# Layer A's attention: the value products that close a unit are issued ahead of a step's scores

## The chip, the cores and the metric

The kernel runs on one core of a Trainium2 chip. The metric is the device time of one execution in microseconds (us). Three runs of the kernel before gave 2460.7 (median), 2458.39 and 2463.78 us.

## The reference, cut to what matters

The reference is a two-layer decoder trunk over 2048 tokens of width 1024. The change lies in the first layer's attention: 16 heads of width 64, causal, with a learned forget gate whose cumulative logarithm is added to the logits:

```python
logits = einsum('bqhd,bkhd->bhqk', qi, k) * scale
logits = logits + ci[..., :, None] - c_k[..., None, :]
logits = where(causal, logits, -inf)
p = softmax(logits, axis=-1)
out = einsum('bhqk,bkhd->bqhd', p, v)
```

Before it stands a projection of the normed input to queries, keys, values, forget logits and a gate; after it the gated output projection and the second layer.

## The kernel before, in words

All products are made with fp32 operands split into a high and a low part. The first layer's attention is a generator, `attention_a`. Its work is cut into **units**, one for each head and each chunk of 512 queries: 16 heads by 4 chunks is 64 units. A unit of chunk ch (0 to 3) has 2·ch + 2 **steps** of two key blocks of 128, so the chunks have 2, 4, 6 and 8 steps, a head has 20 and all heads 320. The last two steps of a unit lie on the diagonal and are masked; the very last one is only 256 + 128 queries wide.

For each step n the main loop (L1132 on) issues, in this order:

1. `ahead(target - 1)` and later `ahead(target)`: **max pieces** for a chunk about 14 steps on. A piece is one or two products on TensorE (L936) into the tile `mx`, of which there is one, and a row maximum on VectorE: L952 for the first half of a long row, L947 (with the mask, and a short read of the accumulator) for the second. The four maxima of a chunk go by DMA into a row of the query operand (L560). There are 24 pieces to a head, so a step has one, or now and then two.
2. `scores(n)`: four products (L984, L985) into two of three `sc` banks, on diagonal steps the mask products (L989, L993); the exponential on ScalarE (L990, L999); its high part, also on ScalarE (L1002); the low part by a subtraction on GpSimd (L1003); and sums of the exponentials into `ac` on VectorE (L1012; at the first step of a unit a ScalarE copy, L1006, takes the place of one addition; at its end L897 reduces `ac`).
3. `values(...)` of the oldest pending step, three steps back (`V_LAG = 3`): four products (L1027) of the high and low parts with the values, which add up in the one `pa` bank over the unit. The last `values` of a unit also issues the **output copy** from `pa` on ScalarE (L1035) and two DMAs on SyncE's queue that store it (L1037, L1038). Only when the copy is over can the next unit's first value product write to `pa`.
4. `recips`, five steps after a head's end: a small product (L906) and its reciprocals.
5. `feed`: some products of the SiLU gate's projection (L1066) into the `pb` bank, which fill up TensorE.

So after a unit's last step k, its closing values are issued at step k + 3, and the first values of the next unit at step k + 4. By the chunk that ends, step k + 3 is the third step of chunk 1 (after chunk 0), the third step of chunk 2, the third step of chunk 3, and, after chunk 3, the first step of chunk 1 of the next head.

Each engine works through its own queue in order. The order in the queues is laid down when the program is built, by and large in the order of issue, with what was not expected to be ready moved back. `sq` has two buffers, shared by the output copy, the gate's results and the reciprocals.

Of the kernel before, what the change touches and what calls it, by code (L numbers as in the profile page):

```python
# [40 lines left out]
V_LAG = 3  # L41
# [57 lines left out]
def f_(ap):  # L99
    return ap.bitcast(F32)  # L100
# [51 lines left out]
class Trunk:  # L152
# [696 lines left out]
    def attention_a(self, op):  # L849
# [19 lines left out]
        units = [(h, ch) for h in range(H) for ch in range(NCH)]  # L869
# [24 lines left out]
        def sums(u):  # L894

            h, ch = units[u]
            nc.vector.tensor_reduce(  # L897
                part[:, h % 2, ch, :], state[u][0].rearrange("p (b i) -> p b i", i=32),
                AX.X, ALU.add, apply_transpose=True,
            )  # L900

        def recips(h, c0=0, c1=NCH):

            nr = (c1 - c0) * NSB
            ps = self.ps("sc", [nr, 32])
            nc.tensor.matmul(  # L906
                ps, part[:, h % 2, c0:c1].rearrange("p c b -> p (c b)"), self.fold,
                start=True, stop=True,
            )
            rc = self.sb("sq", [nr, 32])  # L910
            nc.vector.tensor_tensor(rc, ps, roots[:nr, 1 if c0 else 0], ALU.mult)
            nc.vector.reciprocal(rc, rc)
            nc.sync.dma_start(
                out=d["rd"][h, c0 * CH : c1 * CH].rearrange("(b i) -> b i", i=32), in_=rc
            )
# [44 lines left out]
        def blocks(ch, p):  # L960

            if p < 2 * ch:
                return [(2 * p, 0, 512, 0), (2 * p + 1, 0, 512, 512)]
            if p == 2 * ch:
                return [(2 * p, 0, 512, 0), (2 * p + 1, 128, 384, 512)]
            return [(2 * p, 256, 256, 0), (2 * p + 1, 384, 128, 256)]

        def scores(n, u, p):
            h, ch = units[u]
            ka, kb, qa, qb, v, _ = heads[h]  # L970
            bl = blocks(ch, p)
            diag, last = p >= 2 * ch, p > 2 * ch

            tiles = [self.ps("sc", [P, CH]) for _ in range(1 if last else 2)]
            tw = bl[1][3] + bl[1][2]
            pf = self.sb("st", [P, 1024])
            ph, pl = pht[:, n % 4, :], plt[:, n % 4, :]
            for n_, (k, q0, w, off) in enumerate(bl):
                qs = slice(ch * CH + q0, ch * CH + q0 + w)
                ks = slice(k * P, (k + 1) * P)  # L980
                ps = tiles[0 if last else n_]
                o0 = off if last else 0
                o = ps[:, o0 : o0 + w]
                nc.tensor.matmul(o, ka[:, ks], qa[:, qs], start=not (last and n_), stop=False)  # L984
                nc.tensor.matmul(o, kb[:, ks], qb[:, qs], start=False, stop=not diag)  # L985

            if last:
                o = tiles[0].rearrange("p (b q) -> p b q", b=2)[:, :, :P]
                nc.tensor.matmul(o, self.identb, self.mask_s, start=False, stop=True)  # L989
                nc.scalar.activation(pf[:, :tw], tiles[0][:, :tw], AF.Exp, scale=HD**-0.5)  # L990
            else:
                for n_, ps in enumerate(tiles if diag else ()):
                    mm = nc.tensor.matmul(  # L993
                        ps[:, :P], self.identb, self.mask_s[:, 0], start=False, stop=True
                    )
                    if n_:
                        tc.keep_in_program_order(mm)
                for ps, (k, q0, w, off) in zip(tiles, bl):
                    nc.scalar.activation(  # L999
                        pf[:, off : off + w], ps[:, :w], AF.Exp, scale=HD**-0.5  # L1000
                    )
            nc.scalar.copy(ph[:, :tw], pf[:, :tw])  # L1002
            nc.gpsimd.tensor_tensor(pl[:, :tw], pf[:, :tw], f_(ph[:, :tw]), ALU.subtract)  # L1003
            if p == 0:
                state[u] = [self.ps("ac", [P, CH]), None]
                nc.scalar.copy(state[u][0], pf[:, :CH])  # L1006
            acc = state[u][0]
            for n_, (k, q0, w, off) in enumerate(bl):
                if p == 0 and n_ == 0:
                    continue  # L1010
                a_ = acc[:, q0 : q0 + w]
                nc.vector.tensor_tensor(a_, a_, pf[:, off : off + w], ALU.add)  # L1012
            if last:
                sums(u)
            return (u, p, ph, pl)

        def values(item):
            u, p, ph, pl = item
            h, ch = units[u]
            v = heads[h][4]  # L1020
            if p == 0:
                state[u][1] = self.ps("pa", [P, CH])
            pv = state[u][1]
            last = p == 2 * ch + 1
            for n_, (k, q0, w, off) in enumerate(blocks(ch, p)):
                for i, src in enumerate((ph, pl)):
                    nc.tensor.matmul(  # L1027
                        pv[:, q0 : q0 + w], v[:, k, :], src[:, off : off + w],
                        start=(p == 0 and n_ == 0 and i == 0),
                        stop=(last and n_ == 1 and i == 1),  # L1030
                    )
            if last:
                state.pop(u)
                ov = self.sb("sq", [P, CH])
                nc.scalar.copy(ov, pv)  # L1035
                rows, cols = slice(h * HD, (h + 1) * HD), slice(ch * CH, (ch + 1) * CH)
                nc.sync.dma_start(out=d["om"][rows, cols], in_=ov[:HD, :])  # L1037
                nc.sync.dma_start(out=d["oc"][rows, cols], in_=ov[HD:, :])  # L1038

        def gate_weights(ft, dt):  # L1040
            w = self.sb(next(weight_slots), [P, 2, 2, 2, P], F32R)
            nc.sync.dma_start(out=f_(w), in_=d["wg"][ft, :, dt // 2 : dt // 2 + 2])
            return w
# [39 lines left out]
        def more_pieces(n):  # L1083
            nonlocal loaded
            while len(pieces) < n and loaded < H:
                load_max(loaded)
                if loaded:
                    load_rest(loaded)
                for ch in range(NCH):
                    pieces.extend(max_pieces(loaded, ch))  # L1090
                loaded += 1
# [8 lines left out]
        def ahead(target):  # L1100
            nonlocal done
            while done < min(target, len(pieces)):
                pieces[done]()
                done += 1
# [11 lines left out]
        def feed(n, pause=False):  # L1116


            nonlocal fed, rest
            if pause and rest:  # L1120
                rest = False
                return
            while fed < min(total, n):
                next(filler, None)
                fed += 1
                if pause and fed % (3 * NDT) == 0:
                    rest = True
                    break

        pending, due = [], []  # L1130

        for n, (u, p) in enumerate(steps):  # L1132
            h, ch = units[u]
            if n % per_head == LOAD_AT and h + 1 < H:
                more_pieces(len(pieces) + 1)
            target = per * (n + AHEAD + 1) // per_head + 1
            ahead(target - 1)
            pending.append(scores(n, u, p))
            ahead(target)
            if len(pending) > V_LAG:  # L1140
                values(pending.pop(0))
            if p == 2 * ch + 1:
                if h == H - 1 and ch in (0, NCH - 1):
                    due.append((n + SUM_LAG, (h, ch and 1, ch + 1)))
                elif ch == NCH - 1:
                    due.append((n + SUM_LAG, (h,)))
            while due and due[0][0] <= n:
                recips(*due.pop(0)[1])
            feed((total - KEPT) * (n + 1) // len(steps), pause=True)
            if n == RAW_AT:  # L1150
                raw = self.sb("big", [P, NDT // 2, D])
                for p in range(NDT // 2):
                    op.weight_load(p, raw[:, p])
            if n in PREP_AT:
                op.load(PREP_AT.index(n), ("qn", "wh", "qn", "wl"))
                op.prepare(PREP_AT.index(n), nc.gpsimd)
# [466 lines left out]
```

## Time and profile before

| | |
|---|---|
| median of the runs | 2460.7 us (2458.39 to 2463.78) |
| profiled execution, first to last instruction | 2459.7 us |
| its main attention stage | about 599 to 1462 us |
| TensorE (PE) busy | 2424.1 us, 12016 products |
| weight loads (PEld) busy | 2022.4 us |
| VectorE (DVE) busy | 1727.4 us |
| ScalarE (ACT) busy | 1255.1 us |
| GpSimd (POOL) busy | 1001.9 us |
| TensorE clock granted, mean | 0.999 |

The profile gives one row for each group of instructions: source line, engine, operation, output and input tiles, shape, count, then busy time, mean duration, and the idle time of the engine ahead of them with what ended most of it. A product is given from its start to a modelled end, and the next one may start before that end; so the distance between two starts, not the length, is what a product takes of TensorE's time. A timeline row merges like instructions that follow each other (x4 is four of them) and states the start, the length to the end of the last, and, in brackets, idle time and who ended it.

### The profile page before, as it was taken

The page shows a single profiled execution, that of the slowest core. Times are in us where ns is not written, and L with a number is a line of the kernel's source. Part 1 is how long each engine was busy: PE and PEld are TensorE (multiplying, and loading weights), DVE is VectorE, ACT ScalarE, POOL GpSimd, SP SyncE. Part 2 cuts the span into 40 slices and gives each one's busy share as a digit, 9 for nine tenths or more (in the row PEclk, how much of TensorE's full clock was granted, in tenths as well). Part 3 has the DMA queues.
Part 4 walks back from the last instruction along what each step waited for, and adds up shares of the span by engine and source line. Part 5 has one row for each costly group of instructions (what it writes and reads, how often), then busy time and mean ns, then how long its engine had stood idle before and what let it go on. Part 6 is the DMA issues. An engine that isn't in the chain of part 4 may idle for free.

```text
span 2459.7 us, 36240 instructions
## 1 busy us (share of the span) xinstructions
PE 2424.1 (99%) x12016; PEld 2022.4 (82%) x12016; DVE 1727.4 (70%) x3826; ACT 1255.1 (51%) x2504; POOL 1001.9 (41%) x643
## 2 busy tenths in 40 slices
PE   8999999999999999999999999999999999999999
PEld 6788899988888887878877778888788888888887
DVE  7656567735888888888888866456766523777776
ACT  5433324323777777777777761135323312555554
POOL 0000000012877777777778862210011000377775
PEclk9999999999999999999999999999999999999999
DMA  6656545687554655465456649975434415555552
GB/s 181 207 165 193 156 145 168 192 261 223 168 155 128 210 141 150 143 198 164 133 168 182 169 137 306 290 253 153 139 90 120 137 64 165 174 176 178 180 180 73
DMA packets 351515, 419.24 MB, mean 170 GB/s; under 512 B 64928, under 2 KB 248256, under 8 KB 345152
## 3 DMA queue, kind: packets, MB, share of 16 engines
q1 hardware_dynamic: 351328, 416.92, 56.6%
q8 instruction: 95, 1.56, 0.3%
q14 instruction: 92, 0.75, 0.1%
HBM read 265.29 MB, written 151.40 MB: 169 GB/s over the span
## 4 chain that ended last, share of the span: by engine, by line
PE 46%; DVE 4%; DMA 2%; ACT 2%; POOL 2%; issue 2%; SPq 0%; DVEq 0%; ACTq 0%; POOLq 0%
PE b L759 9%; PE b L1240 5%; PE pa L1027 5%; PE pb L1453 4%; PE pb L722 3%; PE pb L1066 3%; PE b L722 3%; PE mx L936 2%; PE sc L985 2%; PE sc L984 2%; PE pa L1383 1%; PE b L1304 1%; PE pa L722 1%; PE pa L1240 1%; PE pb L1240 1%
## 5 line engine op out<-in xcount | busy, mean ns | idle before, releaser
L759 PE MATMUL b<-wh,big 128*128 128x512 f32 (+3 forms) x2560 | 770.1, 375 | 9.8 <-ACT wh L486 8.7
L1003 POOL TENSOR_TENSOR big<-st,big 128x1024 fp32r<-128x1024 f32 (+1 forms) x320 | 657.9, 2070 | 261.4 <-ACT big L1002 155.6
L759 PEld LDWEIGHTS b<-wh,big 128*128 128x128 f32 x2560 | 471.3, 188 | 81.2 <-ACT wh L486 10.5
L759 PE MATMUL b<-wl,big 128*128 128x512 f32 (+3 forms) x1280 | 474.2, 371 | 1.9 <-DVE wl L487 1.9
L1012 DVE TENSOR_TENSOR ac<-ac,st 128x512 f32<-128x512 f32 (+3 forms) x576 | 355.4, 617 | 55.6 <-ACT st L999 27.2
L999 ACT ACTIVATE st<-sc 128x512 f32<-128x512 f32 (+1 forms) x512 | 274.3, 585 | 161.8 <-PE sc L985 79.0
L1027 PE MATMUL pa<-big 128*128 128x512 f32 (+3 forms) x1280 | 326.1, 369 | 3.9 <-POOL big L1003 1.8
L1002 ACT CAST big<-st 128x1024 fp32r<-128x1024 f32 (+1 forms) x320 | 295.6, 924 | 7.8
L759 PEld LDWEIGHTS b<-wl,big 128*128 128x128 f32 x1280 | 241.4, 189 | 38.3 <-DVE wl L487 6.1
L1027 PEld LDWEIGHTS pa<-big 128*128 128x128 f32 x1280 | 222.0, 189 | 50.3 <-ACT sq L1035 17.0
L947 DVE CUSTOM_DVE_ANT_0 mx<-mx,rot 128x128 f32<-128x128 f32 (+3 forms) x240 | 210.7, 878 | 40.9 <-PE mx L936 34.8
L495 ACT ACTIVATE sq<-b,r 128x512 f32<-128x512 f32 (+2 forms) x128 | 77.8, 608 | 301.6 <-PE b L759 298.6
L984 PE MATMUL sc<-big 128*128 128x512 f32 (+3 forms) x640 | 230.1, 364 | 1.3 <-DVE st L542 1.1
L985 PE MATMUL sc<-big 67*128 67x512 f32 (+3 forms) x640 | 229.0, 367 | 0.0
L936 PE MATMUL mx<-big 66*128 66x128 f32 (+3 forms) x660 | 191.1, 363 | 3.6 <-DVE mt L947 3.1
L1066 PE MATMUL pb<-wh,wr 128*128 128x512 f32 x488 | 179.3, 398 | 2.8 <-DMA wr<-wg 2.2
L859 POOL MEMSET rot<- 128x1024 bf16 x1 | 1.0, 952 | 420.8 <-PE pb L349 420.8
L497 DVE TENSOR_REDUCE sm<-sq 128x8 f32<-128x512 f32 (+2 forms) x128 | 74.9, 585 | 138.6 <-ACT sq L495 138.4
L1352 POOL TENSOR_TENSOR big<-big,tri 128x1024 fp32r<-128x1024 f32 x60 | 143.8, 2397 | 67.1 <-DVE big L1349 62.2
L936 PEld LDWEIGHTS mx<-big 66*128 66x128 f32 x660 | 114.1, 190 | 40.9 <-DVE mt L947 11.9
L984 PEld LDWEIGHTS sc<-big 128*128 128x128 f32 x640 | 121.0, 189 | 23.1 <-DVE st L542 1.5
L985 PEld LDWEIGHTS sc<-big 67*128 67x128 f32 x640 | 121.2, 189 | 21.0
(281 smaller groups left out, 4124.8 us busy)
## 6 DMA issues: line engine op xcount, KB each, us to landing
wr<-wg SPq DMA_DIRECT2D x62, 512.0 KB
va<-st SPq DMA_DIRECT2D x32, 512.0 KB
ka<-st SPq DMA_DIRECT2D x64, 256.0 KB
ut<-big SPq DMA_DIRECT2D x16, 1024.0 KB
big<-ka SPq DMA_DIRECT2D x16, 1024.0 KB
big<-qa SPq DMA_DIRECT2D x16, 1024.0 KB
qb<-st SPq DMA_DIRECT2D x64, 256.0 KB
big<-qb SPq DMA_DIRECT2D x16, 1024.0 KB
```

The source lines that it names most:

```text
L722: nc.tensor.matmul(ps, W[k][dt][:, ft * P : (ft + 1) * P], u[ch][:, dt, :], start=(dt == 0 and i == 0), stop=(dt == NDT - 1 and i == 2),)
L759: nc.tensor.matmul(ps[:, :n], u[tb // 4][:, dt, us], W[k][dt], start=(dt == 0 and i == 0), stop=(dt == NDT - 1 and i == 2),)
L936: mm = nc.tensor.matmul(ps[:, b, :wb], qb[:66, i * P : (i + 1) * P], kb[:66, k0 + b * wb : k0 + (b + 1) * wb], start=True, stop=True,)
L947: nc.vector.tensor_tensor_reduce(out=lg, in0=lg, in1=mask, scale=1.0, scalar=NEG, op0=ALU.add, op1=ALU.max, accum_out=f_(o),)
L984: nc.tensor.matmul(o, ka[:, ks], qa[:, qs], start=not (last and n_), stop=False)
L985: nc.tensor.matmul(o, kb[:, ks], qb[:, qs], start=False, stop=not diag)
L999: nc.scalar.activation(pf[:, off : off + w], ps[:, :w], AF.Exp, scale=HD**-0.5)
L1002: nc.scalar.copy(ph[:, :tw], pf[:, :tw])
L1003: nc.gpsimd.tensor_tensor(pl[:, :tw], pf[:, :tw], f_(ph[:, :tw]), ALU.subtract)
L1012: nc.vector.tensor_tensor(a_, a_, pf[:, off : off + w], ALU.add)
L1027: nc.tensor.matmul(pv[:, q0 : q0 + w], v[:, k, :], src[:, off : off + w], start=(p == 0 and n_ == 0 and i == 0), stop=(last and n_ == 1 an ...
L1066: nc.tensor.matmul(ps, w[:, dt // 2 % 2, wk, dt % 2, :], us[dt][uk], start=(dt == 0 and i == 0), stop=(dt == NDT - 1 and i == 2),)
```

## The change

A helper `closes(item)` says whether a pending step is the last of its unit. Where three steps are pending and the oldest closes its unit, `values` of it now runs between `ahead(target - 1)` and `scores(n)`; on those steps nothing is popped after the scores. On all other steps the order stays. The unit that ends with the last step of all is still closed in the loop after the main one, so 63 of 64 closings are moved, each with its four products, the output copy and the two DMAs. No instruction is added or taken away.

```diff
+        def closes(item):
+            u, p = item[:2]
+            return p == 2 * units[u][1] + 1
+
...
             target = per * (n + AHEAD + 1) // per_head + 1
             ahead(target - 1)
+            ends = len(pending) == V_LAG and closes(pending[0])
+            if ends:
+                values(pending.pop(0))
             pending.append(scores(n, u, p))
             ahead(target)
-            if len(pending) > V_LAG:
+            if len(pending) > V_LAG and not ends:
                 values(pending.pop(0))
```

## The prediction

> **What bounds the kernel now.** I read the page first, then the stage by windows, then the waits of that stage, then the timeline around one closing of each kind. The page:
>
> ```profile
> span 2459.7 us, 36240 instructions
> PE 2424.1 (99%) x12016; PEld 2022.4 (82%) x12016; DVE 1727.4 (70%) x3826; ACT 1255.1 (51%) x2504; POOL 1001.9 (41%) x643
> ```
>
> The main attention stage alone, as a window (us, PE, PEld, DVE, ACT, POOL busy):
>
> ```profile
> 599.00:1462.00 863.00, 852.58 (x4150) 689.13 (x4149) 737.16 (x1362) 661.88 (x1055) 668.41 (x329) 1.00 0.56 162
> ```
>
> TensorE bounds the stage: VectorE is busy 85% of it, GpSimd and ScalarE 77%. But 852.58 of 863 us doesn't mean that only 10.4 us are left. The timeline below has a product of 0.39 us whose successor starts 0.23 us later (759.29 and 759.52): the modelled ends overlap, and a gap shorter than 0.16 us doesn't show as idle. So I measure by distances between starts: 0.23 us for 512 columns. [...] By the busy time the change could bring 10.4 us at the very most, by the starts more; the working goes by the starts.
>
> Who makes TensorE's weight loads wait in this stage (us in total, times, longest):
>
> ```profile
> PEld pa L1027 <- ACT sq L1035: 17.0, 51, 0.7
> PEld mx L936 <- DVE mt L947: 11.9, 26, 1.0
> PEld mx L936 <- DVE m L947: 9.3, 24, 0.5
> PEld mx L936 <- DVE mt L952: 3.7, 19, 0.4
> ```
>
> The first row is what the change aims at: in 51 of the 63 transitions the first value product of a unit waits for the output copy of the unit before. The other three, 24.9 us, are the max pieces, which wait until VectorE has emptied the one `mx` tile. They decide how much of the gain stays.
>
> **What the present wait costs.** After chunk 3 (TensorE, then ScalarE):
>
> ```profile
> 758.19 0.57 PE L936 MATMUL mx<-big 66*128 66x448 f32 x2
> 758.60 0.58 PE L1027 MATMUL pa<-big 128*128 128x256 f32 x4
> 759.01 0.45 PE L1066 MATMUL pb<-wl,wr 128*128 128x512 f32 x1
> 759.29 0.39 PE L1066 MATMUL pb<-wh,wr 128*128 128x512 f32 x1
> 759.52 0.39 PE L984 MATMUL sc<-big 128*128 128x512 f32 x1
> ...
> 760.46 0.60 PE L936 MATMUL mx<-big 66*128 66x480 f32 x2
> 761.05 1.08 PE L1027 MATMUL pa<-big 128*128 128x512 f32 x4
> 761.98 0.39 PE L1066 MATMUL pb<-wh,wr 128*128 128x512 f32 x1
> ```
>
> ```profile
> 757.97 1.09 ACT L999 ACTIVATE st<-sc 128x512 f32<-128x512 f32 x2 [1.57 <-PE sc L985]
> ...
> 759.46 1.06 ACT L1002 CAST big<-st 128x1024 fp32r<-128x1024 f32 x1
> 760.41 0.59 ACT L1035 COPY sq<-pa 128x512 f32<-128x512 f32 x1
> ```
>
> The closing products start at 758.60 and the gate's follow at 759.01, yet the copy starts at 760.41, because in ScalarE's queue it stands behind this step's exponentials and high part. It ends at 761.00, and the next unit's value products start at 761.05. The two 448-column max products took 0.41 us, so two of 480 need 0.44; here 0.59 passed, 0.15 lost. The four value products (512, 512, 384, 384 columns) need 0.23·3.5 = 0.81, and 0.93 passed: another 0.12, weight loads that have to catch up. Lost: 0.27 us.
>
> After chunk 2:
>
> ```profile
> 1281.85 0.43 PE L936 MATMUL mx<-big 66*128 66x288 f32 x2
> 1282.12 0.57 PE L1027 MATMUL pa<-big 128*128 128x256 f32 x4
> ...
> 1283.98 0.45 PE L936 MATMUL mx<-big 66*128 66x320 f32 x2
> 1284.35 1.20 PE L1027 MATMUL pa<-big 128*128 128x512 f32 x4
> 1285.39 0.39 PE L1066 MATMUL pb<-wh,wr 128*128 128x512 f32 x1
> ```
>
> The 288 pair took 0.27, so the 320 pair needs 0.30 and had 0.37; four full value products need 0.92 and had 1.04. Lost: 0.19 us. After chunk 1:
>
> ```profile
> 774.49 0.34 PE L936 MATMUL mx<-big 66*128 66x384 f32 x1
> ...
> 776.53 0.40 PE L936 MATMUL mx<-big 66*128 66x512 f32 x1
> 776.99 1.21 PE L1027 MATMUL pa<-big 128*128 128x512 f32 x4
> 778.04 0.62 PE L1066 MATMUL pb<-wh,wr 128*128 128x512 f32 x2
> ```
>
> One full max product needs 0.23 and had 0.46; the value products 0.92 and had 1.05. Lost: 0.36 us. After chunk 0:
>
> ```profile
> 872.32 0.68 PE L936 MATMUL mx<-big 66*128 66x480 f32 x2
> ...
> 874.59 0.71 PE L936 MATMUL mx<-big 66*128 66x512 f32 x2
> 875.14 1.09 PE L1027 MATMUL pa<-big 128*128 128x512 f32 x4
> 876.07 0.39 PE L1066 MATMUL pb<-wh,wr 128*128 128x512 f32 x1
> ```
>
> Value products at 0.93, as they should be; nothing lost to the copy (the 0.09 in front lies between the two max products). A head so loses 0.27 + 0.19 + 0.36 + 0 = 0.82 us, 16 heads 13.1. The row of waits has 51 instead of 63, so I scale: 13.1·51/63 = 10.6 us. Upper bound 17.0, the row itself; it counts idle time of the load queue that isn't always TensorE's.
>
> **What the change moves.** The four closing products go ahead of the scores, some 1.33 us earlier (from 758.60 to where the scores now start: 758.19 less four products of 0.23, which is 757.27). Three things follow.
>
> Their operands. The last low part of a unit is a 384-wide subtraction, the second of this row, so it ended at 1275.53 for the closing at 1282.12:
>
> ```profile
> 1272.45 3.08 POOL L1003 TENSOR_TENSOR big<-st,big 128x896 fp32r<-128x896 f32 x2 [0.94 <-PE mx L936]
> ```
>
> That leaves 6.6 us; 1.33 less costs nothing. If it did, the whole step's scores would stand behind it.
>
> The copy. It now stands ahead of the step's exponentials on ScalarE. After chunk 3 ScalarE was idle for 1.57 us before 757.97, so the copy runs as soon as the closing products are through: start 757.27 + 0.41, and some 0.3 until the last has drained (an estimate: that group of four is 0.58 long against 0.41 to the next start, and I add 0.1 for the release), so 757.98 to 758.57. The first exponential would be ready at 757.97 + 0.46 (the closing products now in front) = 758.43 and waits 0.14 us. The next unit's values come at 761.05: 2.5 us after the copy's end. So the wait goes entirely, as long as the copy doesn't get behind other work. The pay is the exponential: behind it on ScalarE stand the second one and the high part, and behind that the subtraction on GpSimd; their values are due three steps later, with the same several us in hand. The two DMAs on SyncE's queue come earlier too, with their copy; they pass only that step's late max rows (L560), which wait for VectorE anyway, so nothing is held behind them that wasn't. I count nothing for them. [...]
>
> The max pieces. This is the debit. Before, the closing products stood between the piece of this step and that of the next; now they don't, so between the two pieces TensorE has 0.46 us less (0.41, and the 0.05 by which the gate product behind them was late). In this time VectorE must empty `mx`. VectorE's rows after chunks 3, 2, 1 and 0:
>
> ```profile
> 759.81 0.14 DVE L947 DVE_READ_ACCUMULATOR2_ANT mt<- 128x1 f32 x1
> ```
>
> ```profile
> 1282.28 0.70 DVE L1012 TENSOR_TENSOR ac<-ac,st 128x512 f32<-128x512 f32 x1 [0.53 <-ACT st L999]
> ...
> 1283.56 0.14 DVE L947 DVE_READ_ACCUMULATOR2_ANT mt<- 128x1 f32 x1
> ```
>
> ```profile
> 775.71 0.14 DVE L947 DVE_READ_ACCUMULATOR2_ANT m<- 128x1 f32 x1
> ```
>
> ```profile
> 874.12 0.14 DVE L947 DVE_READ_ACCUMULATOR2_ANT mt<- 128x1 f32 x1
> ```
>
> Counted from the start of a piece: after chunk 3 the tile is empty 1.76 us later (759.95 - 758.19), and the next piece comes after 760.46 - 758.19 - 0.46 = 1.81. Just in time. After chunk 1: empty after 1.36, next after 1.58; in time. After chunk 2: empty after 1.85, next after 2.13 - 0.46 = 1.67: late by 0.18, some 0.1 more for the exponential that VectorE's addition waits for (the 0.53), and 0.12 for the loads to catch up: 0.4 us. After chunk 0: empty after 1.94, next after 2.27 - 0.46 = 1.81: late by 0.13, with 0.12 of catching up 0.25 us. So if the order in the queues stays as it is, 16·(0.4 + 0.25)·51/63 = 8.4 us come back as waits of the max pieces, and 2.2 remain.
>
> But the order need not stay. When a piece isn't expected to be ready, what is ready goes first, and now the next unit's value products are ready there, since the copy is long over. The trace has this where values are free:
>
> ```profile
> 1002.68 0.40 PE L1027 MATMUL pa<-big 128*128 128x512 f32 x1
> 1002.92 0.63 PE L936 MATMUL mx<-big 66*128 66x512 f32 x2
> 1003.38 0.86 PE L1027 MATMUL pa<-big 128*128 128x512 f32 x3
> ```
>
> A single value product put ahead gives the piece 0.23 us, which covers most of both lags. I take it that half to two thirds of the 8.4 us are avoided this way: 10.6 - 3.5 = 7.1 us gained. The value lies between 2.2 (none avoided) and 10.6 (all), with the upper bound of the waits 17.0.
>
> So the changed execution would span 2459.7 - 7.1 = 2452.6 us. The median of the runs is 1.0 above the profiled execution, so 2460.7 - 7.1 = 2453.6; I state **2453.6**. A measurement of this kernel can tell about 0.2% from no change, 4.9 us here, so faster begins below 2455.8.
>
> **The rivals.**
>
> *The wait moves to `mx` and takes nearly all.* 2.2 us or less are left: 2458.5. For it: VectorE's lags above, and the 24.9 us that pieces wait already. Against: 69 waits (26 + 24 + 19) stand against some 360 pieces that the stage issues (24 a head, less the 24 issued early), so mostly the order suits VectorE. Chance 0.24.
>
> *VectorE's late emptying costs more than the copy did: slower.* The place is the addition at 1282.28, which stands ahead of the reduction and itself waits for the exponential. If the copy pushes the exponentials by the 0.6 us that it lasts instead of 0.14, every kind of closing gets late: after chunks 2 and 0 0.5 more, after chunks 1 and 3 about 0.4 (0.22 and 0.05 in hand, 0.12 to catch up): 0.9 + 0.75 + 0.4 + 0.57 = 2.6 a head, where 0.82 are saved; even a third of that surplus, 0.6 us a head, gives +9.6 us, 2470. It decides from 0.82 us a head on, 0.20 a closing. Against it: ScalarE is idle just before these exponentials (1.57 and, after chunk 2, released by TensorE's scores). Chance 0.11.
>
> *No debit at all:* the copy's wait goes and pieces step back everywhere: 10.6 to 13.1 us, 2449. Chance 0.17.
>
> *The change doesn't do what it says:* the scores are expected to be ready first and stay ahead, and all is as before, 2460.7. With 6.6 us in hand for the operands this is unlikely. Chance 0.05.
>
> **How the numbers follow.** The forecast has 0.43. Its own range is 2450 to 2457, of which a good part ends below 2455.8. Faster: 0.17 + 0.36 of the forecast = 0.53. Same: 0.07 of it, 0.24, 0.05 = 0.36. Slower 0.11, of which the mild end lies below 2466. For 8 in 10 I go from 2447 (the 13.1 us) to 2462.5, which leaves out the far end of the copy's bound (17.0) and the slower case.
>
> **What would show it.** Right: the copy (L1035) starts within about 0.5 us of the closing products' end and ahead of the step's exponentials; the wait of L1027 for L1035 falls from 17.0 us to under 2; waits of L936 for VectorE rise from 24.9 to about 28 to 30; the stage's 863 us shrink by some 7. Single steps are wrong if L1027 begins to wait for L1003 (the operands), if L984 waits for L999, or if the rows of `mx` grow by more than 10 us; the prediction as a whole is wrong if the copy's wait goes and the span still doesn't fall by 5 us.

## The result, and the profile after

The changed kernel took 2452.91 us (median of 5 runs, 2452.36 to 2455.11); the kernel before, run beside it, 2461.68 (2458.39 to 2463.78). The ratio is 0.9969, with a 95% interval of 0.9957 to 0.9982: faster by 0.3%, 8.8 us between the medians. The forecast was 2453.6, 7.1 us below the 2460.7 that it started from.

The changed page begins so:

```profile
span 2450.4 us, 36233 instructions
PE 2414.6 (99%) x12016; PEld 2021.7 (83%) x12016; DVE 1724.2 (70%) x3826; ACT 1259.4 (51%) x2504; POOL 1000.4 (41%) x643
```

The span is 9.3 us shorter than that of the profiled execution before. The lines of the gate's products have moved from L1066 to L1070; the last of them shows where the attention stage ends. Before, then after (start of the first, start of the last):

```profile
L1066 PE MATMUL pb<-wh,wr x488: 387/393/502, 595.8 to 1471.7; 128*128 128x512 f32 x163
```

```profile
L1070 PE MATMUL pb<-wh,wr x488: 387/393/504, 595.9 to 1463.2; 128*128 128x512 f32 x163
```

So 8.6 of the 9.3 us come out of this stage, 875.9 to 867.3. What the weight loads wait for in it, after the change:

```profile
PEld mx L936 <- DVE mt L947: 18.4, 49, 0.9
...
PEld mx L936 <- DVE m L947: 8.2, 28, 0.5
PEld pb L1070 <- DMA wr<-wg: 7.1, 7, 2.4
...
PEld pa L1027 <- POOL big L1003: 3.5, 6, 1.4
PEld mx L936 <- DVE mt L952: 2.8, 16, 0.3
PEld sc L984 <- ACT st L999: 2.8, 9, 0.6
PEld pa L1027 <- ACT sq L1035: 1.0, 2, 0.5
```

The wait for the output copy, 17.0 us in 51 places before, is 1.0 in two. The max pieces' three rows were 24.9 and are 29.4 (18.4 + 8.2 + 2.8). Two other rows have grown: the gate's weights wait 7.1 us for their DMA (3.5 before), the scores 2.8 us for an exponential (1.2 before).

The closing after chunk 2 of the same head as in the prediction, on TensorE and on ScalarE:

```profile
1273.39 0.57 PE L1027 MATMUL pa<-big 128*128 128x256 f32 x4
1273.80 0.45 PE L984 MATMUL sc<-big 128*128 128x512 f32 x1
...
1274.79 0.43 PE L936 MATMUL mx<-big 66*128 66x288 f32 x2
...
1276.44 0.40 PE L1027 MATMUL pa<-big 128*128 128x512 f32 x1
1276.68 0.56 PE L936 MATMUL mx<-big 66*128 66x320 f32 x2
```

```profile
1272.74 1.05 ACT L1002 CAST big<-st 128x1024 fp32r<-128x1024 f32 x1
1274.00 0.59 ACT L1035 COPY sq<-pa 128x512 f32<-128x512 f32 x1 [0.20 <-PE pa L1027]
1274.58 1.09 ACT L999 ACTIVATE st<-sc 128x512 f32<-128x512 f32 x2
```

The closing products start at 1273.39 and the copy at 1274.00, 0.61 us later (before the change 1.61, from 1282.12 to 1283.73). It ends at 1274.59, the exponentials follow at once, and the next unit's first value product comes at 1276.44, 1.85 us after the copy's end, with no wait. And one value product stands ahead of the max piece at 1276.68, which before the change came first (1283.98, then values at 1284.35).

### The profile page after: what moved, and what is told of

It is laid out like the page before. It is cut to its first block, busy times and chain, and to the rows that moved or that the text cites. A ratio compares the mean times of both kernels' runs of the same rounds, so it can differ in the third digit from the quotient of the medians.

```text
span 2450.4 us, 36233 instructions
## 1 busy us (share of the span) xinstructions
PE 2414.6 (99%) x12016; PEld 2021.7 (83%) x12016; DVE 1724.2 (70%) x3826; ACT 1259.4 (51%) x2504; POOL 1000.4 (41%) x643
## 4 chain that ended last, share of the span: by engine, by line
PE 80%; DVE 6%; DMA 4%; ACT 4%; issue 3%; POOL 3%; SPq 0%; DVEq 0%; ACTq 0%; POOLq 0%
PE b L759 27%; PE pa L1027 9%; PE pb L1070 7%; PE b L1247 5%; PE mx L936 5%; PE sc L984 5%; PE sc L985 5%; PE pb L722 3%; PE b L722 3%; PE pb L1460 2%; DMA wr<-wg 1%; POOL big L1359 1%; ACT st L1330 1%; PE pb L349 1%; PE pa L349 1%
## 5 line engine op out<-in xcount | busy, mean ns | idle before, releaser
L1012 DVE TENSOR_TENSOR ac<-ac,st 128x512 f32<-128x512 f32 (+3 forms) x576 | 356.0, 618 | 52.4 <-ACT st L999 28.6
L1070 PE MATMUL pb<-wh,wr 128*128 128x512 f32 x488 | 178.9, 397 | 4.4 <-DMA wr<-wg 4.3
L936 PEld LDWEIGHTS mx<-big 66*128 66x128 f32 x660 | 113.2, 190 | 43.8 <-DVE mt L947 18.4
L1247 PE MATMUL b<-big 128*128 128x512 f32 x576 | 135.9, 389 | 1.5 <-DVE sq L1079 1.5
```

What stands on the lines that cost most here:

```text
L936: mm = nc.tensor.matmul(ps[:, b, :wb], qb[:66, i * P : (i + 1) * P], kb[:66, k0 + b * wb : k0 + (b + 1) * wb], start=True, stop=True,)
L1070: nc.tensor.matmul(ps, w[:, dt // 2 % 2, wk, dt % 2, :], us[dt][uk], start=(dt == 0 and i == 0), stop=(dt == NDT - 1 and i == 2),)
L1247: nc.tensor.matmul(bank[tb][nh], op.y(s_)[:, k, tb * P : (tb + 1) * P], op.W[p_][:, j, nh * CH : (nh + 1) * CH], start=(p_ == 0 and i == 0 ...
```

## The experiments

Twelve kernels ran, in four jobs; the kernel before, run beside them, had medians of 2461.55 (the first four), 2459.85 (the next four), 2459.89 (the short copies) and 2460.22 us (the halved sums).

Each run also has its mean granted TensorE clock, here 0.997 to 1.000. Within one kernel, less clock goes with more time: of the kernel before, in the first job, 11 runs at 1.000 have a mean of 2460.0 us and 16 at 0.999 one of 2462.6. Some of the kernels below were granted less clock than the kernel before, and why stays open; where that matters, the means of the runs at 0.999 stand beside the medians.

### Is it the copy or the order of the products? The copy held back

```diff
 if ends:
-    values(pending.pop(0))
+    store = values(pending.pop(0), defer=True)
 pending.append(scores(n, u, p))
 ahead(target)
+if ends:
+    store()    # copy, kept in program order, and its DMAs
```

> The closing value products stay early, but the output copy is issued after the step's scores and pinned behind the step's high part on ScalarE, where it stood before the change. Theory (the gain is the copy's wait): the copy is late again, the weight loads of the value products wait for it 12 to 20 us again (1.0 after the change, 17.0 before), and the time is that of before or a little more, 2459 to 2465 us. Rival (the gain comes from TensorE's changed order, whatever the copy does): 2451 to 2455 us, as after the change.

Measured: 2466.85 us, ratio 1.0023 (1.0014 to 1.0031), slower than before. The waits:

```profile
PEld mx L936 <- DVE mt L947: 19.5, 50, 0.9
PEld mx L936 <- DVE m L947: 12.7, 33, 0.5
...
PEld pa L1027 <- ACT sq L1035: 8.6, 29, 0.8
```

The theory's side holds: without the early copy the gain isn't just lost, it turns into a loss of 5.3 us, even more than I allowed (3.2 us at the same clock: four runs at 0.999 have a mean of 2465.8, the 16 of the kernel before 2462.6). The row is below the 12 to 20 us that I gave, for a reason that the timeline of this run shows at one closing (after chunk 3): the late copy was allowed for when the queues were laid down, and gate products were put ahead of the values.

```profile
981.78 0.60 ACT L1035 COPY sq<-pa 128x512 f32<-128x512 f32 x1
```

```profile
981.92 0.40 PE L1076 MATMUL pb<-wh,wr 128*128 128x512 f32 x1
...
982.62 1.38 PE L1027 MATMUL pa<-big 128*128 128x512 f32 x8
```

### Values early on every step

```diff
-ends = len(pending) == V_LAG and closes(pending[0])
+ends = len(pending) == V_LAG
```

> The oldest pending values go ahead of the scores on every step, not only on closing ones. Theory: the copy's wait is gone as after the change (under 2 us), and since values now stand between any two max pieces alike, the waits of the max pieces for VectorE fall from 29.4 us (after) to below before's 24.9; the time is 2448 to 2452 us. Rival (operands: values a third of a step earlier on all steps wait for GpSimd's low part): the loads' wait of the value products for the low part rises from 3.5 us to 10 or more and the time is 2456 us or more.

Measured: 2472.15 us, 1.0044 (1.0032 to 1.0056). My theory missed by 20 us; the rival had the right row:

```profile
PEld pa L1027 <- POOL big L1003: 18.7, 31, 2.0
PEld mx L936 <- DVE mt L947: 10.3, 26, 0.6
PEld mx L936 <- DVE m L947: 10.2, 31, 0.7
...
PEld pa L1027 <- ACT sq L1035: 9.0, 22, 1.3
PEld mx L936 <- DVE mt L952: 8.1, 38, 0.4
```

Values of ordinary steps now wait for GpSimd's low part (18.7 us, 3.5 in the changed kernel). The copy's wait is half back too (9.0), since the next unit's first values are now early as well, so that the copy has less time. The pieces' waits, 28.6, fell by 0.8 only. Of the two sets tried, the closings are the one that can be early.

### Which closings carry the gain

```diff
-ends = len(pending) == V_LAG and closes(pending[0])
+ends = len(pending) == V_LAG and closes(pending[0]) and units[pending[0][0]][1] == 0
```

and, the other way round, the same with `> 0`.

> Only the closings after chunk 0 are early, the other 47 stay where they were. Theory: there the copy cost TensorE nothing, so there is nothing to gain, and the piece that follows gets late: 2460 to 2465 us, the copy's wait at 14 to 15 us. Rival (TensorE's changed order): about a quarter of the gain, 2458 to 2460 us.

> The closings after chunks 1, 2 and 3 are early, those after chunk 0 stay. Theory: all of the gain, with a little less debit, 2449 to 2453 us; the copy's wait is about 2 to 3 us, all of it after chunk 0. Rival (TensorE's changed order): three quarters of the gain, 2454 to 2457 us.

Measured: chunk 0 alone 2461.23 us, 1.0004 (0.9995 to 1.0013), no difference from before, with the copy's row at 15.4; chunks 1 to 3 2455.52 us, 0.9976 (0.9968 to 0.9985), the copy's row at 3.7. So the gain that shows is that of the closings after chunks 1 to 3, as the four samples of the prediction had it (0.36, 0.19, 0.27 and 0 us). But 2455.52 lies in the range that I gave for the rival (2454 to 2457), not in the theory's (2449 to 2453); what speaks against the rival is the other run, where its quarter of the gain didn't come. Whether chunk 0 adds anything on top of the others can't be told: the intervals of 0.9976 and of the full change, 0.9969, overlap.

### The slower rival: a longer copy

```diff
 nc.scalar.copy(ov, pv)
+nc.scalar.copy(ov, pv)
```

> The changed kernel with the output copy done twice, one right after the other, at all 64 closings: 0.58 us more of ScalarE's time ahead of the exponentials, the result the same. The slower rival of the prediction (exponentials pushed by the copy's length make VectorE empty the max tile late at every closing): 1.8 us a head, up to 29 us, at least 10 us slower than the changed kernel, 2463 us or more, with the max pieces' waits at 40 us or more. My theory now (pieces step back behind value products, and ScalarE has idle time there): 1 to 5 us slower than the changed kernel, 2454 to 2458 us, the pieces' waits between 29 and 36 us.

Measured: 2457.63 us, 0.9991 (0.9982 to 1.0000). By the medians that is 4.7 us over the changed kernel, inside my range and far from 2463; part of it is clock, 0.9985 in the mean against 0.9998: at 0.999 seven runs have a mean of 2456.1 us, and the one run of the changed kernel took 2454.85. The pieces' rows sum to 28.7 (18.6 + 7.1 + 3.0), no more than the 29.4 of the single copy; the rows that grew are other ones, the values' wait for GpSimd (6.8, from 3.5) and for the copy itself (2.8, from 1.0).

But the run tests the rival less than the edit suggests. The second copy doesn't depend on the step's scores, and in 47 of the 63 closings it went into ScalarE's queue behind the step's first exponential, as here:

```profile
755.85 0.59 ACT L1035 COPY sq<-pa 128x512 f32<-128x512 f32 x1 [1.44 <-PE pa L1027]
756.42 0.60 ACT L999 ACTIVATE st<-sc 128x512 f32<-128x512 f32 x1
756.92 0.58 ACT L1036 COPY sq<-pa 128x512 f32<-128x512 f32 x1
```

So 64·0.58 = 37 us more on ScalarE cost 4.7 us by the medians, clock included, but in most places they didn't hold up the first exponential. What a first exponential pushed by a second copy would cost isn't shown.

### The copy early on ScalarE, the products late on TensorE

```diff
-def scores(n, u, p):
+def scores(n, u, p, mid=None):
...
+    if mid is not None:
+        mid()          # values(...) of the closing step
     for ps, (k, q0, w, off) in zip(tiles, bl):
         nc.scalar.activation(
```

> On closing steps the closing products and the copy are issued between the step's score products and its exponentials: TensorE does the scores first, as before the change, and only the copy comes ahead on ScalarE, to between the exponentials and the high part. Theory (the place of the copy in ScalarE's queue is what counts, the place of the products on TensorE only as far as it lets the copy start): the copy's wait is under 6 us, the time 2452 to 2457 us. Rival (the products must be ahead on TensorE): 2459 us or more.

Measured: 2465.25 us, 1.0019 (1.0009 to 1.0028), in the rival's range. The copy's row is 13.0 us in 27 places, and the pieces' rows sum to 31.4 (19.5 + 9.6 + 2.3):

```profile
PEld mx L936 <- DVE mt L947: 19.5, 58, 0.7
PEld pa L1029 <- ACT sq L1037: 13.0, 27, 0.7
```

ScalarE and TensorE of this run at a closing after chunk 2 (the value products are L1029 here, the copy L1037, the high part L1004):

```profile
1010.93 1.05 ACT L1004 CAST big<-st 128x1024 fp32r<-128x1024 f32 x1
1011.89 0.57 ACT L1037 COPY sq<-pa 128x512 f32<-128x512 f32 x1
```

```profile
1010.02 0.57 PE L1029 MATMUL pa<-big 128*128 128x256 f32 x4
...
1012.52 0.50 PE L1029 MATMUL pa<-big 128*128 128x512 f32 x1 [0.21 <-ACT sq L1037]
```

At this closing the copy still stands behind the high part, and so it does in 34 of the 63. In the other 29 it went ahead of the high part, as meant (7 before the change); after chunk 3 it started 1.28 us after the closing products' start (median; 1.81 before, 0.61 after the change). So the copy got the place that was meant for it in under half of the closings, the next values still waited for it, and the run doesn't settle what an early copy behind late products would bring. It does show that this order doesn't bring the gain; nor did the early products with the late copy above.

### The copy issued behind the exponentials, without a pin

```diff
 if ends:
-    values(pending.pop(0))
+    store = values(pending.pop(0), defer=True)
 pending.append(scores(n, u, p))
 ahead(target)
+if ends:
+    store()
```

> The closing products are early as in the changed kernel, the copy is issued after the step's scores without a pin, and so stands behind the exponentials and ahead of the high part. Theory: the copy still ends before the next unit's values (wait under 4 us), the exponentials are not held up, and the max pieces wait a little less than the 29.4 us of the changed kernel: 2450 to 2455 us. Rival (from the late pinned copy, 2466.9 us: early products cost by themselves, and only a copy ahead of the exponentials makes up for it): 2457 us or more.

Measured: 2451.31 us, 0.9968 (0.9956 to 0.9981). This tells less than it seems: the copy doesn't depend on the scores, and when the queues were laid down it went back ahead of the exponentials in 57 of 63 closings (61 in the changed kernel). The pieces' rows of the profile are those of the changed kernel but for 0.1 (18.4, 8.1, 2.9). It is a repeat of the changed kernel, and a good one: 0.9968 against 0.9969.

### The piece between the closing products and the scores

```diff
 if ends:
     values(pending.pop(0))
+    ahead(target)
 pending.append(scores(n, u, p))
```

> The changed kernel, but on closing steps the max piece is issued between the closing products and the scores, so that the distances between pieces are more even (about 1.9 and 2.3 us instead of 2.8 and 1.8) and VectorE's reduction stands ahead of the additions. Theory (the debit is the piece that comes too soon after the closing step): the pieces' waits fall from 29.4 us to 20 to 26, and the time is 2446 to 2451 us. Rival (the scores, and with them the exponentials and sums, then come late by a piece, and VectorE's additions hold up the next piece instead): 2452 us or more, the pieces' waits at 28 us or more.

Measured: 2454.82 us, 0.9981 (0.9972 to 0.9990). The pieces' rows fell to 24.7 as expected:

```profile
PEld mx L936 <- DVE mt L947: 11.7, 28, 0.6
...
PEld mx L936 <- DVE m L947: 9.0, 25, 0.6
...
PEld mx L936 <- DVE mt L952: 4.0, 20, 0.5
```

but the time didn't; by the ratios it is 0.12% above the changed kernel, with overlapping intervals. So the sum of these rows isn't time that can be had back one for one.

### The copy's wait alone: a short copy in both orders

In both, the copy and its stores take 32 of 512 columns, and the output stage reads the gate's result where it read the two stored parts; the change's own lines stand in the second only.

```diff
-nc.scalar.copy(ov, pv)
+nc.scalar.copy(ov[:, :32], pv[:, :32])
...
-nc.sync.dma_start(out=m, in_=d["om"][rows, cols])
+nc.sync.dma_start(out=m, in_=d["gt"][rows, cols])
```

> The kernel before the change, order and all, but the output copy takes 32 of the 512 columns, the two stores take those columns alone, and the output stage reads the gate's result in their place: 480 of 512 columns of the attention's output are left out. Nothing is moved on TensorE, and the copy's 0.58 us shrinks to a fifth or less. Theory (the gain of the change is the time that the first value products wait for the copy, mostly 0.15 to 0.4 us at a time, and the max pieces are its debit): most of the wait goes without a debit, the copy's row falls from 17.0 to under 5 us, the pieces' waits stay at 22 to 28 us, and the attention stage is 8 to 12 us shorter: 2448 to 2453 us. Rival (the gain has to do with TensorE's changed order): the time stays within 3 us of the kernel before, though the wait is gone.

> The changed kernel with the same short copy, the same 480 columns left out. With the copy short in both, what is left between this and the run with the old order is the price of the early closing products by themselves. Theory: the debit, 2 to 6 us slower than the run with the short copy in the old order, with the max pieces' waits 4 us higher or more (29 us or more). Rival (no debit; the early products cost nothing or help by themselves): the same time within 1 us, or faster.

Measured: old order 2456.05 us, 0.9986 (0.9977 to 0.9994); early closings 2453.5 us, 0.9969 (0.9958 to 0.9980). The copy took 0.18 us instead of 0.58, a third and not a fifth. Old order first, then early:

```profile
PEld mx L936 <- DVE mt L947: 13.2, 35, 0.6
...
PEld mx L936 <- DVE m L947: 9.8, 26, 0.8
PEld mx L936 <- DVE mt L952: 7.2, 31, 0.5
...
PEld pa L1027 <- ACT sq L1035: 3.6, 9, 0.6
```

```profile
PEld mx L936 <- DVE mt L947: 18.7, 52, 0.6
PEld mx L936 <- DVE m L947: 10.3, 28, 0.5
...
PEld mx L936 <- DVE mt L952: 2.7, 15, 0.3
```

Two things follow. In the old order, where the source moves no product and only the wait is (mostly) gone, the time falls by 3.8 us by the medians, not the 8 to 12 that I expected. Part of the rest is clock, 0.9984 in the mean against 0.9997: five runs at 0.999 have a mean of 2454.4 us, five of the kernel before 2461.2, 6.8 more. In the profiled execution, also at 0.999, the gate's products run from 597.0 to 1464.7, so the stage is 867.7 us long, 8.2 less than before. So the wait alone, without a product moved, is worth 3.8 of the 6.4 us that the short copy with early closings gains by the medians, and 6.8 of 8.2 at the same clock. And with the short copy the early closings aren't slower than the old order but, if anything, faster (2453.0 at 0.999). So the early products by themselves have no debit that shows in the time. The pieces' rows, 30.2 and 31.7, are nearly the same too, but they aren't the same waits, as the table below shows.

### VectorE relieved

```diff
 for n_, (k, q0, w, off) in enumerate(bl):
-    if p == 0 and n_ == 0:
+    if n_ == 1 or p == 0:
         continue
```

and in `recips` a sum instead of the product ahead of the reciprocal.

> The changed kernel with VectorE relieved: of each step's two additions to the sum of exponentials the second is left out (a good 300 of 576 additions in the stage, 0.3 to 0.7 us each), so the softmax's denominator lacks every second key block, and its reciprocal takes a sum in place of a product. Theory (the debit of the change is TensorE running up against VectorE at the max pieces): the pieces' waits fall from 29.4 us to under 12, and the run is faster than its partner in the old order by more than the 8 to 9 us that the change brings with VectorE loaded, 10 to 13 us. Rival (the pieces' waits aren't what holds the gain back): the difference to the partner stays at 8 us or less.

> The kernel before the change with the same additions left out and the same reciprocal. Theory: the copy's wait stays at 15 us or more, the pieces' waits fall from 24.9 to under 10 us; the time is 2450 to 2458 us, and the partner with early closings is 10 to 13 us faster. Rival: the partner is 8 us faster or less.

Measured: early 2461.72 us, 1.0004 (0.9995 to 1.0013); old order 2462.98 us, 1.0008 (1.0000 to 1.0017). VectorE's busy time in the stage fell from 737 us (before) and 736 (after the change) to 575 (old order) and 572 (early), and neither kernel got faster than before (at a clock of 0.999 the means are 2460.7 early, 2461.0 in the old order and 2462.0 before). Early, then old order:

```profile
PEld mx L936 <- DVE mt L947: 22.2, 64, 0.6
PEld mx L936 <- DVE m L947: 11.6, 36, 0.5
PEld pb L1070 <- DMA wr<-wg: 11.1, 6, 2.9
...
PEld mx L936 <- DVE mt L952: 2.5, 15, 0.2
```

```profile
PEld pa L1027 <- ACT sq L1035: 17.4, 55, 0.7
PEld mx L936 <- DVE mt L947: 13.9, 33, 0.6
...
PEld mx L936 <- DVE m L947: 9.2, 21, 0.5
...
PEld mx L936 <- DVE mt L952: 2.0, 12, 0.3
```

The pieces' waits are 36.3 and 25.1: they don't fall with VectorE's load. Some come from a chain. VectorE in the early kernel, at a closing after chunk 2:

```profile
952.73 0.70 DVE L1012 TENSOR_TENSOR ac<-ac,st 128x512 f32<-128x512 f32 x1 [1.60 <-ACT st L999]
953.34 0.76 DVE L947 CUSTOM_DVE_ANT_0 mx<-mx,rot 128x576 f32<-128x576 f32 x1
954.01 0.14 DVE L947 DVE_READ_ACCUMULATOR2_ANT mt<- 128x1 f32 x1
```

VectorE stood idle for 1.60 us and then did the addition ahead of the reduction, because the addition stands first in its queue and waits for the exponential; the max tile was empty at 954.15, 1.83 us after its piece (952.32), where before the change it was 1.85. Leaving out other additions can't help there.

That chain is the smaller part. By the trace of the early kernel it stands behind 26 of the 115 waits (6.7 of 36.3 us). In 78 of them (26.4 us) VectorE was idle until the piece's products were through, began the reduction at once, and the next piece came before it was over; in the changed kernel these are 55 of 93 (18.9 us). There the distance of two pieces on TensorE and the length of one reduction count (0.76 us above), and the edit touches neither.

Where the pieces wait, taken from the traces piece by piece (places that wait, us; the first column is the first piece from the scores of the step after a closing step on, which there is in 51 to 60 of the 63 closings, and where the prediction put its debit):

| kernel | piece after a closing step | all other pieces |
|---|---|---|
| before | 6, 2.0 | 63, 22.9 |
| changed | 37, 10.1 | 56, 19.4 |
| short copy, old order | 4, 1.2 | 88, 29.0 |
| short copy, early | 36, 11.4 | 59, 20.3 |
| halved sums, old order | 6, 2.5 | 60, 22.7 |
| halved sums, early | 35, 9.4 | 80, 26.9 |
| piece ahead of the scores | 5, 1.9 | 69, 23.0 |

In all three pairs the early closings bring 7 to 10 us of waits at that one piece. What the other pieces do differs from pair to pair.

The pair has a second lesson. The values' wait for the copy goes from 17.4 us to nothing that shows among the rows, and the time only by 1.3 us. The pieces took 11.2 back (25.1 to 36.3), and the gate's weights wait for their DMA 2.9 us more (8.2 to 11.1). In this kernel the rival "the wait moves to `mx` and takes nearly all" is what happens.

## Why the prediction was right, point by point

**The bound.** TensorE, by distances between starts and not by busy time: right. Busy time in the stage left 10.4 us; the stage shrank by 8.6 and is still stretched by the waits above. That the stated time came out within 0.7 us is in part luck: the fall was 8.8 us where I had 7.1, and the kernel before ran 1.0 us slower beside the changed one than in the runs that I started from.

**The wait and its price.** Right. The row went from 17.0 to 1.0, with the copy 0.6 us after the closing products' start where I had worked out 0.7 (757.27 to 757.98). In that estimate I had added 0.1 us for the release, which no trace shows: in the view after the change the copy starts 0.04 us after the modelled end of the four products (1273.96 and 1274.00). The late copy, the short copy and the chunk runs show that the gain hangs on this wait: hold the copy back and it is gone, shorten the copy and over half of it comes without a product moved, and the closings without a wait bring nothing. The price of 10.6 us by itself wasn't measured; the nearest is the short copy in the old order, 3.8 us by the medians, 6.8 at the same clock and 8.2 in the profiled stage, with 3.6 of the 17.0 us of waits left.

The wait rests on engines that work through their queues in order. The trace of the kernel before has it for three of them. VectorE stood idle for 1.11 us until 1260.79 because of a step of the gate (L1073), though the piece whose reduction came next (1259.22) was through at 1259.62. ScalarE stood idle for 0.34 us until 1261.52, again for the gate (L1074), though the first score products of the exponential that came next were through at 1260.78. And TensorE's loads stood idle for 0.40 us until 761.05 for the copy, though the gate's product that came after the values (761.98) has nothing to do with it. For GpSimd and SyncE it is not shown here.

**The operands.** Right for the closings: the wait for GpSimd is 3.5 us after and was 3.3 before. The run with all steps early shows that the margin belongs to the closings alone.

**The exponential behind the copy.** Right in kind. After chunk 3 the first exponential comes 0.78 us after the step's first score product (756.85 and 757.63), before the change 0.72 (757.25 and 757.97): 0.06 us late where I had 0.14. The sign that I named against this step shows a little: the scores' wait for the exponential went from 1.2 to 2.8 us.

**The debit at the max pieces.** The place was right, and the size in part luck. I worked out 8.4 us for the piece after the closing step if the order stayed, and took 3.5 of it. That piece has 8.1 us more of load waits (10.1, from 2.0), though the detour that I counted on was there, a value product ahead of the piece (1276.44 and 1276.68), in 43 of 60 places (one of 56 before). The other pieces wait 3.5 us less, for which I had no term, and only so does the sum rise by 4.5. By the chunk: after chunk 2, forecast late, 14 of 15 pieces wait (4.4 us); after chunk 0, forecast late, none does, with the detour in all 15; after chunk 3, forecast just in time, 13 wait (3.9 us), and yet the product comes as I had it, 1.81 us after the piece before (757.84 and 759.65). So the wait of a load isn't yet a late product. What the debit cost in time stays open: the short copy shows none, and the run with the piece ahead of the scores took most of these waits away (1.9 us left) and was no faster.

Why a saved wait comes back at the pieces in part in one kernel (4.5 of 16.0 us of load waits here) and nearly whole in another (the halved sums) stays open: each of these kernels has its queues laid down anew, and the rows of load waits don't add up to TensorE's time, as the run with the piece ahead of the scores showed.

**The DMAs.** I counted nothing for them, and the gate's weights wait 3.6 us more for theirs (3.5 to 7.1). With the short copy that wait is 4.9 us in the old order and 3.2 with early closings, so the early closings alone don't explain it; the cause stays open.

**The rivals.** *The wait moves to `mx`*: by the sum of the rows 4.5 of 16.0 us here, nearly all with the halved sums. *Slower by the exponentials*: not seen in the change, where the copy stands ahead of both exponentials in 61 of 63 closings; the second copy tested it only in part. *No debit at all*: the pieces' rows rose by 4.5 us and the time fell by 8.8, less than the 10.6 us of that case. *The order is kept as it was*: not so, the closings are early in the queues.

## What to carry to other kernels

When a product waits for a copy that empties its accumulator, look where the copy stands in its engine's queue and what stands ahead of it; here the last products went ahead on TensorE so that the copy could go ahead on ScalarE, and that brought 0.3%; with the copy held back the same early products ended 0.2% slower. Don't take such a row of waits for time: about half of it was (8.6 of 17.0 us), while other waits grew behind it (4.5 us at the max pieces, 3.6 at the gate's weights). And look for work that may come early at no price among the steps with the longest wait for their operands, here the closings (6.6 us in hand), not the ordinary steps.

## What the runs showed of the hardware that was not expected

A good fifth less of VectorE's work in the stage (165 of 737 us of busy time) changed nothing for the better in the time that TensorE waits for VectorE: most of these waits (26.4 of 36.3 us) fell where VectorE had been idle until the piece came, so that the length of one reduction (0.76 us above) counted, or where an addition stood ahead of the reduction and waited itself (6.7 us), and not how busy VectorE was. And in this program the idle time of the weight loads is a poor measure of TensorE's time: 4.7 us less of it at the max pieces (29.4 to 24.7) went with a time that was no shorter.
